# A matrix product in seven block products instead of eight, and a norm applied ahead of the transposes

## The chip, the cores and the metric

One core of one Trainium2 chip runs the whole program. The metric is device time in microseconds (us) of one execution; the kernel before takes 893.79 us in the median of three runs (893.76 to 894.05). The engines are TensorE (PE in the profile: matmuls and transposes, its weight loads are PEld), VectorE (DVE), ScalarE (ACT), GpSimd (POOL) and the queues that issue transfers (SP above all).

## The reference

The program is one encoder layer on 512 tokens of width 1024: a token mixer with recurrent head groups, a cross-attention over 256 memory tokens, and a squared-ReLU MLP, each added to the residual stream, then a final RMSNorm. What the change touches is the last third:

```python
def rmsnorm(x, g):
    y = x32 * lax.rsqrt(jnp.mean(x32 * x32, axis=-1, keepdims=True) + NORM_EPS)
    return y * g
...
x = x + cross_attention(...)                    # ends in  o @ w_xo
n = rmsnorm(x, norm_mlp)                        # 512 x 1024
x = x + jnp.square(jax.nn.relu(n @ w_up)) @ w_down   # w_up 1024 x 4096, w_down 4096 x 1024
return rmsnorm(x, norm_final)
```

## The kernel before

Everything is float32. A product is made of three matmuls on a split of each operand into a rounded high part and a low rest: high x high, high x low, low x high (`mm3`, L221 to L224). The split of a weight tile of 128 x 1024 is one copy on ACT (`wh`, L218) and one subtraction on DVE (`wl`, L219). Weight tiles come by DMA in the order of a list (`SEQ`) into three `st` buffers; `wh` and `wl` have three buffers each, so the split of tile n waits until PE has read tile n-3. `weights` splits two tiles ahead, with a raised priority.

The residual stream is held as eight tiles `xr[t, c]` (`vv` in the profile): four token tiles t of 128 tokens, two column halves c of 512. `proj_t` computes token-major tiles: four PSUM tiles (`mm`) are accumulated side by side for one column half. `proj_d` computes feature-major tiles: 128 features x 512 tokens, 24 matmuls each.

The part around the change runs so:

- **xo projection** (`proj_res`, L753): for each column half, `proj_t` yields the four token tiles; each is added to the stream on DVE (L757), squared and summed on ACT (`stats`, L751), transposed on PE in four blocks (L765) into one PSUM tile `sm`, and split into `xT` by ACT and DVE (L770, L771), scaled by the norm's gain. The factor 1/rms per token is not applied there. It commutes with ReLU, so its square (`r2`, one reciprocal at L852) is multiplied in when the MLP's output is added to the stream (L888).
- **MLP in four quarters** (L865): quarter f computes 1024 of the 4096 features, eight `proj_d` tiles of the up matrix (the *up stage*, 192 matmuls). Each is passed through ReLU on ACT (L873), squared on DVE (L874) and split (L218, L219). Then the *down stage*: `proj_t` with eight weight tiles of the down matrix, two column halves, 192 matmuls, and four additions to the stream per half (L888).
- **The end**: in the last quarter, the sums of squares, the power -0.5 on POOL (L164), the final scale and gain (L858, L861) and the output transfers.

A scheduler sets the order on each engine when the program is built. An engine takes its instructions in that order.

## Time and profile before

| | |
|---|---|
| median of the runs | 893.79 us |
| the profiled execution's own time | 895.82 us |
| its span (first to last instruction) | 894.0 us |
| PE busy | 875.6 us, 98% of the span |
| DVE busy | 497.7 us, 56% |
| ACT busy | 371.9 us, 42% |
| POOL busy | 19.5 us, 2% |
| mean granted clock of TensorE | 0.996 |

A busy time of matmuls is a pipelined one: a matmul of 512 columns is shown with some 390 ns, while the next starts 227 ns after it. What counts is the distance from start to start. The granted clock is the share of full speed that the chip allows TensorE; in this execution it is 1.00 except after the last matmul.

### The profile page before, as it was taken

What the parts mean: (1) busy time and instruction counts of PE and PEld (TensorE: products, weight loads), DVE (VectorE), ACT (ScalarE), POOL (GpSimd) and SP (SyncE); (2) the same over time, 40 slices, a digit from 0 to 9 for tenths busy, and PEclk for the clock granted to TensorE, in tenths of its full rate; (3) what the DMA queues carried; (4) which work ended last, traced back from release to release, by engine and by line L of the source; (5) the groups of instructions that cost most, each with busy time, mean ns of one, the idle gap of its engine ahead of it and who ended that gap; (6) DMA issues with size and microseconds to landing.
All of it is one profiled execution on the core that took longest, in us unless ns stands there. A gap on an engine that the chain in (4) does not pass through costs nothing.

```text
span 894.0 us, 11028 instructions
## 1 busy us (share of the span) xinstructions
PE 875.6 (98%) x4290; PEld 727.9 (81%) x4290; DVE 497.7 (56%) x863; ACT 371.9 (42%) x701; POOL 19.5 (2%) x49
## 2 busy tenths in 40 slices
PE   7999999999999999999999999999999999999996
PEld 5887888888886987888888888888888888888885
DVE  5557688679346987644555446433444344334443
ACT  5235443353358567544444445322332133114432
POOL 1000000010010000000000000000000000000001
PEclk9999999999999999999999999999999999999999
DMA  6332222312142223422212222322222233332212
GB/s 255 133 100 71 71 71 73 117 59 73 48 141 72 96 95 112 149 94 94 71 48 71 71 94 87 103 95 95 95 94 95 95 98 101 103 100 95 94 48 95
DMA packets 24614, 84.21 MB, mean 94 GB/s; under 512 B 2865, under 2 KB 2993, under 8 KB 24562
## 3 DMA queue, kind: packets, MB, share of 16 engines
q1 hardware_dynamic: 24272, 83.04, 27.5%
q8 instruction: 34, 0.56, 0.3%
q10 hardware_dynamic: 290, 0.47, 0.1%
q14 instruction: 18, 0.15, 0.1%
HBM read 81.40 MB, written 2.10 MB: 93 GB/s over the span
## 4 chain that ended last, share of the span: by engine, by line
PE 67%; DVE 1%; ACT 1%; issue 0%; POOL 0%; POOLq 0%; ACTq 0%
PE mm L223 20%; PE mm L224 20%; PE mm L222 20%; PE sm L626 2%; PE sm L611 2%; PE sm L765 1%; PE sm L223 1%; PE sm L224 1%; PE sm L222 1%; PE sm L822 0%; PE sm L596 0%; DVE wl L219 0%; DVE xT L771 0%; ACT wh L218 0%; POOL tiny L164 0%
## 5 line engine op out<-in xcount | busy, mean ns | idle before, releaser
L219 DVE TENSOR_TENSOR wl<-st,wh 128x1024 fp32r<-128x1024 f32 x141 | 172.6, 1224 | 266.5 <-ACT wh L218 263.1
L218 ACT ACTIVATE wh<-st 128x1024 fp32r<-128x1024 f32 x141 | 149.3, 1059 | 305.2 <-PE mm L224 163.2
L222 PE MATMUL mm<-xT,wh 128*128 128x512 f32 x552 | 220.0, 400 | 0.0
L223 PE MATMUL mm<-xT,wh 128*128 128x512 f32 x552 | 216.6, 392 | 0.2 <-DVE xT L771 0.2
L224 PE MATMUL mm<-xT,wl 128*128 128x512 f32 x552 | 216.8, 393 | 0.0
L224 PEld LDWEIGHTS mm<-xT,wl 128*128 128x128 f32 x552 | 103.9, 188 | 22.3 <-issue 0.6
L222 PEld LDWEIGHTS mm<-xT,wh 128*128 128x128 f32 x552 | 104.2, 189 | 21.7 <-issue 1.4
L223 PEld LDWEIGHTS mm<-xT,wh 128*128 128x128 f32 x552 | 104.2, 189 | 21.6 <-DVE xT L771 0.9
L224 PE MATMUL mm<-wh,yT 128*128 128x512 f32 x256 | 100.4, 392 | 0.0
L222 PE MATMUL mm<-wh,yT 128*128 128x512 f32 x256 | 100.2, 391 | 0.0
L223 PE MATMUL mm<-wl,yT 128*128 128x512 f32 x256 | 99.9, 390 | 0.0
L222 PE MATMUL mm<-wh,a 128*128 128x512 f32 x160 | 63.4, 396 | 0.0
L223 PE MATMUL mm<-wl,a 128*128 128x512 f32 x160 | 62.4, 390 | 0.0
L224 PE MATMUL mm<-wh,a 128*128 128x512 f32 x160 | 62.3, 389 | 0.0
L223 PEld LDWEIGHTS mm<-wl,yT 128*128 128x128 f32 x256 | 48.1, 188 | 9.8
L222 PEld LDWEIGHTS mm<-wh,yT 128*128 128x128 f32 x256 | 48.1, 188 | 9.8
L224 PEld LDWEIGHTS mm<-wh,yT 128*128 128x128 f32 x256 | 48.1, 188 | 9.6
L222 PEld LDWEIGHTS mm<-wh,a 128*128 128x128 f32 x160 | 30.1, 188 | 6.6 <-issue 0.5
L223 PEld LDWEIGHTS mm<-wl,a 128*128 128x128 f32 x160 | 30.1, 188 | 6.5 <-issue 0.5
L224 PEld LDWEIGHTS mm<-wh,a 128*128 128x128 f32 x160 | 30.0, 188 | 6.2
L373 PEld LDWEIGHTS sm<-a,t 128*128 128x128 f32 x224 | 30.1, 191 | 2.2 <-ACT t L363 0.4
L373 PE MATMUL sm<-a,t 128*128 128x128 f32 x224 | 30.9, 285 | 0.0
(222 smaller groups left out, 1110.9 us busy)
## 6 DMA issues: line engine op xcount, KB each, us to landing
st<-in_wpk SPq DMA_DIRECT2D x141, 512.0 KB, 3.2
as<-in_x SPq DMA_DIRECT2D x4, 512.0 KB, 6.4
vv<-in_x SPq DMA_DIRECT2D x8, 256.0 KB, 4.1
out<-vv SPq DMA_DIRECT2D x7, 256.0 KB, 2.2
a<-in_mem SPq DMA_DIRECT2D x2, 512.0 KB, 3.8
t<-in_rows SPq DMA_DIRECT2D x2, 256.0 KB, 5.9
gate<-in_rows SPq DMA_DIRECT2D x1, 512.0 KB, 5.2
a<-in_lmask SPq DMA_DIRECT2D x1, 448.0 KB, 8.3
```

Source lines behind the costliest of these rows:

```text
L218: sc.activation(dst_hi, src, AF.Copy)
L219: v.tensor_tensor(out=dst_lo, in0=src, in1=dst_hi.bitcast(F32), op=ALU.subtract)
L222: pe.matmul(ps, lhsT=ah, rhs=bh, start=first, stop=False)
L223: pe.matmul(ps, lhsT=ah, rhs=bl, start=False, stop=False)
L224: pe.matmul(ps, lhsT=al, rhs=bh, start=False, stop=last)
L373: pe.matmul(ps[:, z], lhsT=kc[:, z], rhs=ap(q2, w * P, [2 * L, P // (2 * L)], [512 + L, 2], [1, L]), start=True, stop=True)
L611: pe.matmul(ps, lhsT=k[:, ws * P:ws * P + P], rhs=q, start=True, stop=True)
L626: pe.matmul(ps[:, dr * 129:dr * 129 + 129], lhsT=St[:, col:col + P], rhs=mv[ws][:, h * 129:h * 129 + 129], start=(i == 0), stop=(i == len( ...
L765: pe.transpose(ps[:, k * P:k * P + P], xr[t, c][:, k * P:k * P + P], ident)
```

## The change

It has two parts.

**The down stage** of a quarter multiplies A (512 tokens x 1024 features) with B (1024 x 1024). A is cut into token halves and feature halves, B into feature halves and output halves. Eight block products of 256 x 512 x 512 become seven (P1 to P7), on sums and differences of blocks:

- S1 = A21 + A22, S2 = S1 - A11, S3 = A11 - A21, S4 = A12 - S2 and T1 = B12 - B11, T2 = B22 - T1, T3 = B22 - B12, T4 = B21 - T2
- P1 = A11 B11, P2 = A12 B21, P3 = S4 B22, P4 = A22 T4, P5 = S1 T1, P6 = S2 T2, P7 = S3 T3
- C11 = P1 + P2; C12 = P1 + P6 + P5 + P3; C21 = P1 + P6 + P7 + P4; C22 = P1 + P6 + P7 + P5

Each P takes 24 matmuls of 512 columns: two token tiles, four feature tiles, three for the split. The four T of a quarter are eight DVE subtractions of 128 x 1024 (L891 of the changed kernel), and B's raw tiles are kept for them; 14 splits of weights (*jobs*, one per P and feature pair) take the place of eight. The four S are four DVE operations of 128 x 256 per feature pair (L980 to L983). Bank X holds P1, then P1 + P6, then P1 + P6 + P7, then the whole of C21, and is read by DVE after each step (L938); Z holds P5, then P5 + P3; Y holds P2. So P6, P3, P7 and P4 wait until DVE has read the bank. The square of the ReLU moves from DVE to ACT (L965).

**The norm**: A mixes tokens of different 1/rms, so the factor can no longer be multiplied in at the end. `proj_res_norm` takes the place of `proj_res` for xo: transposes wait for the second column half, the sum of squares of the whole row, the power on POOL, and the scaling of both halves (DVE for half 0, L788; ACT for half 1, L789). The tail of the second half is `late`: each token tile ends 12 matmuls after the one before (6 in the kernel before). All 16 groups of L768's blocks come at that end, where eight of them (half 0's) lay in the matmuls of half 1 before.

```diff
+    def proj_res_norm(mat, src, tgt, st, pre):
+        for c in range(2):
+            for t, ps in proj_t(mat, 0, 512 * c, src, pre=pre if c == 0 else None, late=c == 1):
+                v.tensor_tensor(out=xr[t, c], in0=ps, in1=xr[t, c], op=ALU.add)
+                stats(st, t, c)
+                if c == 0:
+                    continue
+                s1 = tiny(1)
+                v.tensor_tensor(out=s1, in0=st[:, 2 * t:2 * t + 1], in1=st[:, 2 * t + 1:2 * t + 2], op=ALU.add)
+                r, _ = rstd_of(s1, 1, D)
+                n0, n1 = T2()[:, 0:512], T2()[:, 0:512]
+                v.tensor_scalar(out=n0, in0=xr[t, 0], scalar1=r, scalar2=None, op0=ALU.mult)
+                sc.activation(n1, xr[t, 1], AF.Copy, scale=r)
+                transp(tgt, t, 0, n0)
+                transp(tgt, t, 1, n1)
...
-    proj_res("xo", 0, os_, (x3T, V_MLP), st2, drain)
+    proj_res_norm("xo", os_, (x3T, V_MLP), st2, drain)
...
+    ORDER = ("P1", "P2", "P5", "P6", "P3", "P7", "P4")
+    JOBS = [("P1", 0), ("P2", 0), ("P1", 1), ("P2", 1)] + [(p, g) for p in ORDER[2:] for g in range(2)]
...
+        if p == "P5":
+            sub(b11, b12, b11)
+            return b11
+        if p == "P6":
+            t2 = raw[f, g, "T2"] = A4()[:, :]
+            sub(t2, b22, b11)
+            return t2
+        if p == "P7":
+            sub(b12, b22, b12)
+            return b12
+        sub(b21, b21, raw[f, g, "T2"])
+        return b21
...
+                y = T2()[:, 0:512]
+                sc.activation(y, ps, AF.Relu)
+                sc.activation(y, y, AF.Square)
...
+            v.tensor_tensor(out=s1, in0=x2_, in1=x4, op=ALU.add)
+            v.tensor_tensor(out=s2, in0=s1, in1=x1, op=ALU.subtract)
+            v.tensor_tensor(out=s3, in0=x1, in1=x2_, op=ALU.subtract)
+            v.tensor_tensor(out=s4, in0=x3_, in1=s2, op=ALU.subtract)
...
+        bank = {"P1": X, "P2": Y, "P5": Z, "P6": X, "P3": Z, "P7": X, "P4": X}
+        into = {"P1": [(0, 0)], "P2": [(0, 0)], "P5": [(2, 1)], "P6": [(0, 1)], "P3": [(0, 1)], "P7": [(2, 1)], "P4": [(2, 0)]}
...
+            w = ahead(n)
+            for u in range(2):
+                product(p, g, u, w, g == 0, g == 1)
+                if g == 1:
+                    for t0, c in into[p]:
+                        add_to(t0 + u, c, bank[p][u], fin and p in last)
```

Two places show what the change does to the order of instructions. All engines have the same order up to the tail of the xo projection.

The first is ACT at the end of the xo projection. `vv` is the residual stream, `sm` the PSUM tile of a transpose, `xT` the MLP's input, `st` and `wh` a weight tile and its high part, `t` scratch, `misc` the sums of squares, and `vv_3225` and `vv_3227` are the third and the fourth token tile. In the kernel before:

```order
L751 ACTIVATE t_775_4547,misc<-vv_3225 128x512
L770 ACTIVATE xT_4127<-sm_4505,vc 128x128
L770 ACTIVATE xT_4127<-sm_4527,vc 128x128
L218 ACTIVATE wh_4597<-st_4494 128x1024
L770 ACTIVATE xT_4127<-sm_4505,vc 128x128
L770 ACTIVATE xT_4127<-sm_4527,vc 128x128
L770 ACTIVATE xT_4127<-sm_4549,vc 128x128
L751 ACTIVATE t_777_4569,misc<-vv_3227 128x512
L770 ACTIVATE xT_4127<-sm_4571,vc 128x128
```

In the changed kernel, at the same place:

```order
L220 ACTIVATE wh_4414<-st_4412 128x1024
L773 ACTIVATE xT_4126<-sm_4496,vc 128x128
L773 ACTIVATE xT_4127<-sm_4509,vc 128x128
L220 ACTIVATE wh_4624<-st_4418 128x1024
L753 ACTIVATE t_783_4535,misc<-vv_3225 128x512
L773 ACTIVATE xT_4127<-sm_4509,vc 128x128
L789 ACTIVATE t_788_4544<-vv_3225,tiny_4541 128x512
L753 ACTIVATE t_791_4586,misc<-vv_3227 128x512
L773 ACTIVATE xT_4126<-sm_4547,vc 128x128
L789 ACTIVATE t_796_4595<-vv_3227,tiny_4592 128x512
```

The statistics of the third tile now stand behind two weight splits, of which the second reuses the buffer of the projection's last weight tile, and those of the fourth stand behind the scaling of the third.

The second place is DVE in the down stage of the second quarter (f = 1). `wl` is the low part of a weight tile, `mm` and `sm` are PSUM banks, `a`, `t` and `yT` hold the MLP's activations. In the kernel before, with the end of the up stage:

```order
L219 TENSOR_TENSOR wl_5532<-st_5505,wh_5531 128x1024
L888 SCALAR_TENSOR_TENSOR vv_3213<-mm_5437,misc,vv_3213 128x512
L888 SCALAR_TENSOR_TENSOR vv_3215<-mm_5438,misc,vv_3215 128x512
L888 SCALAR_TENSOR_TENSOR vv_3217<-mm_5439,misc,vv_3217 128x512
L888 SCALAR_TENSOR_TENSOR vv_3219<-mm_5440,misc,vv_3219 128x512
L219 TENSOR_TENSOR wl_5570<-st_5535,wh_5569 128x1024
L219 TENSOR_TENSOR wl_5600<-st_5573,wh_5599 128x1024
```

In the changed kernel, from the split of P1's second job on:

```order
L221 TENSOR_TENSOR wl_5591<-gate_5442,wh_5590 128x1024
L891 TENSOR_TENSOR a_982_5660<-as_5354,as_5265 128x1024
L891 TENSOR_TENSOR gate_5442<-gate_5476,gate_5442 128x1024
L891 TENSOR_TENSOR as_5354<-as_5354,a_982_5660 128x1024
L891 TENSOR_TENSOR a_985_5678<-a_957_5554,gate_5442 128x1024
L891 TENSOR_TENSOR gate_5476<-a_957_5554,gate_5476 128x1024
L221 TENSOR_TENSOR wl_5607<-a_954_5524,wh_5606 128x1024
L221 TENSOR_TENSOR wl_5624<-as_5265,wh_5623 128x1024
L891 TENSOR_TENSOR a_954_5524<-a_954_5524,a_985_5678 128x1024
```

The low part for P2's second feature pair (`wl_5607`) now stands behind five subtractions of raw weights; the additions of P1, P2 and P5 to the stream follow later on the same engine, behind and between five more weight splits, three splits of activations and the last four S.

## Rows read from the trace of the kernel before

**Rows 1.** The page, busy time, share of the span and instructions of each engine.

```profile
PE 875.6 (98%) x4290; PEld 727.9 (81%) x4290; DVE 497.7 (56%) x863; ACT 371.9 (42%) x701; POOL 19.5 (2%) x49
```

**Rows 2.** Timeline of PE (start, duration in us); the last row is the last matmul.

```profile
545.51 0.39 PE L222 MATMUL mm<-xT,wh 128*128 128x512 f32 x1
...
575.43 0.39 PE L222 MATMUL mm<-xT,wh 128*128 128x512 f32 x1
...
885.96 0.39 PE L224 MATMUL mm<-wh,a 128*128 128x512 f32 x1
```

**Rows 3.** All waits of PE from 380 to 886 us: total, times, longest.

```profile
PE mm L223 <- DVE xT L771: 0.2, 1, 0.2
```

**Rows 4.** Timeline from the xo projection's last matmul to the first of up.

```profile
533.76 0.42 PEld L765 LDWEIGHTS sm<-cs,vv 128*128 128x128 f32 x4 [0.31 <-DVE vv L757]
...
537.14 0.48 PE L224 MATMUL mm<-wh,yT 128*128 128x512 f32 x1
...
537.45 0.39 PE L222 MATMUL mm<-xT,wh 128*128 128x512 f32 x1
...
538.39 0.42 PEld L765 LDWEIGHTS sm<-cs,vv 128*128 128x128 f32 x4 [0.29 <-DVE vv L757]
```

**Rows 5.** Groups of instructions by line and shape: busy us, mean ns of one.

```profile
L219 DVE TENSOR_TENSOR wl<-st,wh 128x1024 fp32r<-128x1024 f32 x141 | 172.6, 1224 | 266.5 <-ACT wh L218 263.1 <-PE sm L373 3.3
L218 ACT ACTIVATE wh<-st 128x1024 fp32r<-128x1024 f32 x141 | 149.3, 1059 | 305.2 <-PE mm L224 163.2 <-PE mm L223 107.8 <-issue 31.5
L888 DVE SCALAR_TENSOR_TENSOR vv<-mm,misc,vv 128x512 f32<-128x512 f32 x32 | 23.3, 746 | 13.0 <-PE mm L224 12.8
L757 DVE TENSOR_TENSOR vv<-mm,vv 128x512 f32<-128x512 f32 x16 | 10.6, 683 | 2.3 <-PE mm L224 2.3
L770 ACT ACTIVATE xT<-sm,vc 128x128 fp32r<-128x128 f32 x64 | 20.3, 365 | 4.3 <-DVE xT L771 4.2
L771 DVE SCALAR_TENSOR_TENSOR xT<-sm,vc,xT 128x128 fp32r<-128x128 f32 x64 | 19.5, 345 | 5.8 <-ACT xT L770 5.3
L343 DVE TENSOR_SCALAR a<-a,misc 128x512 f32<-128x512 f32 x8 | 3.8, 480 | 0.0
L858 ACT ACTIVATE vv<-vv,tiny 128x512 f32<-128x512 f32 x4 | 2.8, 712 | 0.9 <-POOL tiny L164 0.9
```

**Rows 6.** Timeline of DVE where it works without a gap.

```profile
299.92 1.21 DVE L219 TENSOR_TENSOR wl<-st,wh 128x1024 fp32r<-128x1024 f32 x1
301.06 0.68 DVE L586 SCALAR_TENSOR_TENSOR yT<-t,t 128x512 f32<-128x512 f32 x1
301.66 0.41 DVE L614 TENSOR_TENSOR as<-as,sm 128x256 f32<-128x256 f32 x1
301.99 0.54 DVE L616 TENSOR_TENSOR as<-as,sm 128x384 f32<-128x384 f32 x1
```

**Rows 7.** Timeline of the end: the norm of a token tile, and an earlier power.

```profile
880.20 0.56 POOL L164 TENSOR_TENSOR tiny<-tiny,misc 128x1 f32<-128x1 f32 x1 [455.49 <-DVE tiny L162]
...
886.39 0.75 DVE L888 SCALAR_TENSOR_TENSOR vv<-mm,misc,vv 128x512 f32<-128x512 f32 x1
887.24 0.63 ACT L751 ACTIVATE t<-vv 128x512 f32<-128x512 f32 x1 [1.38 <-DVE vv L888]
887.77 0.19 ACT L751 ACTIVATION_READ_ACCUMULATOR t<-vv 128x1 f32 x1
...
888.25 0.74 DVE L861 SCALAR_TENSOR_TENSOR vv<-vv,tiny,gate 128x512 f32<-128x512 f32 x1
888.42 0.99 POOL L164 TENSOR_TENSOR tiny<-tiny,misc 128x1 f32<-128x1 f32 x1 [1.73 <-DVE tiny L162]
...
889.44 0.75 DVE L861 SCALAR_TENSOR_TENSOR vv<-vv,tiny,gate 128x512 f32<-128x512 f32 x1 [0.44 <-POOL tiny L164]
```

**Rows 8.** Stretches: from:to and length, busy time of PE, PEld, DVE, ACT, POOL, PEclk, DMA.

```profile
889.50:890.00 0.50, 0.00 (x0) 0.00 (x0) 0.50 (x1) 0.50 (x1) 0.00 (x0) 1.00 1.03 385
...
890.50:891.00 0.50, 0.00 (x0) 0.00 (x0) 0.00 (x0) 0.00 (x0) 0.00 (x0) 0.50 0.57 217
```

More of the change, by code (lines that the diff above doesn't have):

```diff
@@ L65, in _split_order @@
     for f in range(4):
-        seq += d("up", 1024 * f, 8)
-        seq += t("down", 8 * f, 0) + t("down", 8 * f, 512)
+        for j in range(4):
+            seq += d("up", 1024 * f + P * j, 1) + d("up", 1024 * f + P * (j + 4), 1)
+        for g in range(2):
+            seq += [("t", "down", 8 * f + 2 * g + k, c) for k in (0, 4) for c in (0, 512)]
     return seq
@@ L193, in load @@
     def load(i):
-        if i >= len(SEQ) or i in st_tiles:
+        if i >= len(SEQ) or i in st_tiles or SEQ[i][1] == "down":
             return
@@ L200, in split @@
     def split(i):
-        if i >= len(SEQ) or i in hl_tiles:
+        if i >= len(SEQ) or i in hl_tiles or SEQ[i][1] == "down":
             return
@@ L759, in proj_res, with transp @@
                 transp(tgt, t, c)
[L761 removed]
+    def transp(tgt, t, c, src=None):
         dst, gcol = tgt
+        src = xr[t, c] if src is None else src
         ps = smb()
         for k in range(4):
[L765 removed]
+            pe.transpose(ps[:, k * P:k * P + P], src[:, k * P:k * P + P], ident)
         for k in range(4):
@@ new lines, in trunk, with raw_load @@
+    ORDER = ("P1", "P2", "P5", "P6", "P3", "P7", "P4")
+    JOBS = [("P1", 0), ("P2", 0), ("P1", 1), ("P2", 1)] + [(p, g) for p in ORDER[2:] for g in range(2)]
+    raw, jobs_hl = {}, {}
+    def raw_load(f, n):
+        if n == 0 or n == 2:
+            t = A16()
+            raw[f, n], raw[f, n + 1] = t[:, 0:1024], t[:, 1024:2048]
+        elif n >= 4:
+            raw[f, n] = (G4() if n < 6 else A4())[:, :]
+        g, kc = divmod(n, 4)
+        i = SIDX["t", "down", 8 * f + 2 * g + 4 * (kc // 2), 512 * (kc % 2)]
+        nc.sync.dma_start(out=raw[f, n], in_=wpk[i])
@@ new lines, in source @@
+    def source(f, p, g):
+        b11, b12, b21, b22 = [raw[f, 4 * g + n] for n in range(4)]
+        sub = lambda o, a, b: v.tensor_tensor(out=o, in0=a, in1=b, op=ALU.subtract)
+        if p == "P1":
+            return b11
+        if p == "P2":
+            return b21
+        if p == "P3":
+            return b22
+        if p == "P5":
+            sub(b11, b12, b11)
+            return b11
+        if p == "P6":
[6 more added lines that the diff above has]
+        sub(b21, b21, raw[f, g, "T2"])
+        return b21
@@ new lines, in job, with finish @@
+    def job(f, n):
+        if n >= len(JOBS):
+            if f < 3:
+                split(SIDX["d", "up", 0, 1024 * (f + 1)] + n - len(JOBS))
+            return None
+        if (f, n) not in jobs_hl:
+            s_ = source(f, *JOBS[n])
+            hi, lo = T("wh", 1024, 3, F32R), T("wl", 1024, 3, F32R)
+            split_out(hi, lo, s_)
+            jobs_hl[f, n] = (hi, lo)
+        return jobs_hl[f, n]
+    def finish(t, r, first):
+        o = 1 - first
+        sc.activation(xr[t, first], xr[t, first], AF.Copy, scale=r)
+        (nc.scalar if t == 3 else nc.sync).dma_start(out=out[t * P:t * P + P, first * 512:first * 512 + 512], in_=xr[t, first])
+        z = xr[t, o]
+        v.scalar_tensor_tensor(out=z, in0=z, scalar=r, in1=gfin[:, o * 512:o * 512 + 512], op0=ALU.mult, op1=ALU.mult)
+        nc.sync.dma_start(out=out[t * P:t * P + P, o * 512:o * 512 + 512], in_=z)
@@ new lines, in trunk, with add_to @@
+    st3 = misc[:, 42:50]
+    pieces = {}
+    def add_to(t, c, ps, fin=False):
+        z = xr[t, c]
+        v.tensor_tensor(out=z, in0=ps, in1=z, op=ALU.add)
+        if not fin:
+            return
+        stats(st3, t, c)
+        if t not in pieces:
+            pieces[t] = c
+            v.tensor_tensor(out=z, in0=z, in1=gfin[:, c * 512:c * 512 + 512], op=ALU.mult)
+            return
+        s1 = tiny(1)
+        v.tensor_tensor(out=s1, in0=st3[:, 2 * t:2 * t + 1], in1=st3[:, 2 * t + 1:2 * t + 2], op=ALU.add)
+        r, _ = rstd_of(s1, 1, D)
+        finish(t, r, pieces[t])
```

113 lines of the change are left out of this document (63 added, 50 removed).

## The prediction

> **What bounds the kernel now.** I read the page first: PE is busy 98% of the span, DVE 56% and ACT 42% [rows 1]. The share alone could hide a slow PE, so I took its pace from its timeline: between two matmuls 132 apart lie 29.92 us, 0.2267 us each [rows 2]. Then PE's waits: from the xo projection to the last matmul there is one short one of 0.2 us [rows 3], and at the seam between xo and the MLP PE's weight loads wait 0.31 and 0.29 us for the stream's additions [rows 4]. So in this third of the kernel each matmul costs 0.227 us of the end, and other engines cost nothing until they are late. The question is what is late after the change.
>
> **What goes.** A quarter's down stage falls from 192 to 168 matmuls; over four quarters 96 go, and PE's order has exactly 96 rows less. 96 x 0.2267 = 21.8 us. Nothing hides this: PE waited for nothing there. The reciprocal and the multiplication by r2 were never on the path.
>
> **What the norm costs at the seam.** Before, a token tile's way from its last matmul to xT was an addition, four transposes, and eight short copies, under matmuls of its neighbours. Now it is longer, and no up matmul can start before all four token tiles have come through, since each up matmul streams all 512 tokens. I count from the start of the first token tile's last matmul (half 1), 12 matmuls or 2.72 us per tile.
>
> - One tile's chain: the addition starts 0.43 after the last matmul's start (885.96 to 886.39) and the power ends 3.02 later with a power of 0.99 [rows 2, 7]. The power took 0.56 where DVE stood still and 0.99 where L861 ran beside it [rows 7]; DVE will stand waiting for it here, so I take 0.56, and 0.06 less for the plainer addition [rows 5]: 2.5. Scaling takes 0.48 on DVE (like L343) and 0.71 on ACT (like L858) beside it [rows 5].
> - First tile: its transposes can start at 3.5. PE is through the second tile's matmuls at 2.95 and waits 0.55, since the transposes stand next in its order. The second tile's addition stands behind that scaling on DVE; PE waits another 0.7 for it. Transposes of one half hold PE some 0.42 (as in rows 4); the fourth tile's last matmul starts at 11.1 and PE is free at 11.3.
> - Third tile: it was summed long before, but on ACT its statistics stand behind a weight split that reuses the buffer the fourth tile's last matmul reads. That split runs from 11.7 to 12.8 (1.06, rows 5), the statistics to 13.4, DVE's half of the split to 14.0; then addition of the fourth tile, power to 15.8, scaling to 16.5.
> - Fourth tile: statistics 16.5 to 17.2 (ACT was scaling the third tile), power to 18.2, scaling to 18.9, transposes to 19.6. ACT and DVE may not touch one PSUM tile together, so high and low alternate, four PSUM tiles interleaved, 0.37 us per high (0.365, rows 5): the first up matmul gets its data at 20.5, the last low part is there at 25.0. In between PE can do 18 matmuls of the three up tiles whose weights lie ready (4.1 us).
>
> So PE is as far at 24.65 as if it had started at 20.55 without a gap. Its own work to there is 37 matmuls and eight groups of transposes, 11.8 us. The hole is 8.75 us; 0.6 stood there before [rows 4]; cost 8.2. By nearest rows it lies between 5 (each power hidden, splits not in the way) and 11 (every power 0.99 and no overlap between instructions).
>
> **The clock.** PE stands still for some 5 us before the third tile's transposes. At the end of this kernel the granted clock was still 1.00 at 889.5 to 890.0 and 0.50 at 890.5, four us after the last matmul had ended [rows 2, 8]. So at the seam it will probably fall to its lower level (1.2 of 2.4 GHz), and up starts there: a matmul of 0.45 instead of 0.227. No row shows how soon it comes back; I take as long as it took to fall, 4.1 us, in which 9 matmuls are done instead of 18: 2 us. The ends are 0 (it does not fall) and 16 (the first three up tiles, 72 matmuls, at half speed). The Trainium skill (TensorE: Matmul & The Clock Gate, Why this matters for your kernels) tells us to leave no longer idle gaps between bursts of matmuls, since the clock falls back in them; the rows above agree that it falls, and by that rule the seam costs its hole and then a slow start, without it only the hole.
>
> **What the products cost in a down stage.** PE needs per quarter 168 x 0.2267 = 38.1 us. DVE gets in a whole quarter 22 weight splits, 8 subtractions, some 28 smaller operations and 14 additions, about 59 us against PE's 82; as an average it keeps up. But it comes in a lump: P3 overwrites the bank of P5, and the addition that reads it is the 26th instruction from the split of P1's second job on. That split starts 1.1 us after PE's first down matmul, because its buffer comes free with the last up matmul and ACT's half takes 1.06. The 26 are 14 of 128 x 1024, 8 of 512 columns and 4 of 256. One costs 1.22, 0.68 and 0.41 by itself, but back to back they start 1.14, 0.60 and 0.33 apart [rows 5, 6]: 14 x 1.14 + 8 x 0.60 + 4 x 0.35 = 22.2, and with the start 23.3. PE needs for the four products before P3 96 x 0.2267 = 21.8. So PE loses 1.5 us by then. P4 follows P7 in one bank with six matmuls between; its read stands behind two splits on DVE, 0.4. Together 2.0 us per quarter. Bounds: 0.5 (DVE is just in time for P3) and 4.4 (each at its full duration: 25.4 against 21.8, and 0.8 at P4).
>
> In the last quarter DVE has two multiplications by the final gain more before that addition (1.2), one more wait of 0.4 between the two token tiles of P3, and before P4's bank two scalings that wait for POOL (two powers in a row, 1.4 on top): 5.0. At the end the last addition stands behind the scaling of the tile before: 0.5.
>
> The rest is hidden: up stages lose nothing, since PE runs up to four PSUM tiles ahead and each split has one whole tile, 5.4 us, for 2.3 us of work. The square on ACT runs under these matmuls. If that cover went, each late split would cost up to 2.3. DMA moves the same bytes; raw tiles come a stage ahead.
>
> **Sum**, against the profiled execution of 895.8 us (span 894.0, 1.8 around it): -21.8 + 8.2 + 2.0 + 3 x 2.0 + 5.0 + 0.5 = -0.1. The walk lets a waiting engine start 0.05 after its release; from DVE to ACT it is 0.10 (887.14 to 887.24, rows 7), some 20 times over these waits: +1.0. That is +0.9, and since the runs' median is 893.79, 2 below the profiled one, I forecast 894.7 us. Own range of this case: 889 to 901.
>
> **Rivals.**
>
> - *DVE paces the down stages.* The whole of each duration counts, not the shorter distance: 3 x 4.4 + 8 = 21 in place of 11. Then 905. It decides once the 26 instructions take over 24 us. For it: five subtractions stand in one run ahead of a split that PE needs next. Against: DVE's distances in rows 6 hold over 30 us of dense work.
> - *DVE stays ahead and the clock holds.* The additions are in time (0.5 a quarter, 2 in the last), no slow start: -21.8 + 8.2 + 3.5 + 0.5 = -9.6, so 884. For it: the margin is only 1.5 us in 22, and the clock fell only once, four us after all work, here transposes break the gap. Against: the fixed order.
> - *The clock stays low through three up tiles*: 16 instead of 2, 909. For it: in the first microseconds of up, PE waits on xT between matmuls. Against: from 25.0 on it has all data and is dense.
> - *The change does not remove the matmuls, or the scheduler fills the hole*: PE's order shows 96 rows less and nothing but the transposes in the hole. Then 872 would be possible for a filled hole; nearly excluded.
>
> **How the numbers follow.** Forecast case 0.50, DVE as pacer 0.18, DVE ahead 0.27, low clock 0.04, filled hole 0.01. A difference under 0.2% (1.8 us, so 892.0 to 895.6) can't be told from none. Of the forecast case's 0.50, its range gives 0.08 to faster, 0.21 to same, 0.21 to slower; the second rival is faster nearly whole (0.25, 0.02 same), the first and third slower. With the filled hole: faster 0.34, same 0.23, slower 0.43. The range from 883 to 905 takes in the forecast case, nearly all of the second rival and half of the first; 0.18 stays out, most of it above.
>
> **What would show it.** Right, if PE's timeline has a hole of some 8 to 11 us (less its transposes) between xo and up, with a wait for ACT's xT; if the granted clock falls there; if the 24 matmuls saved per quarter come back as waits of 1 to 3 us in each down stage, put down to DVE at the first matmul of P3 and of P4, and of 4 to 6 in the last. Wrong, if a down stage lasts over 43 or under 39 us, if the hole's length hangs on something else than ACT's order, or if the up stages show waits.

## The result, and the profile after

The changed kernel takes 896.13 us in the median of 12 runs (895.04 to 898.79); the kernel before took 894.21 us in the same session (893.76 to 895.36). The ratio is 1.0024, with a 95% interval from 1.0014 to 1.0033: 2.1 us slower. The six runs of 895.04 to 895.72 us have a mean granted clock of 0.993, the six of 896.54 to 898.79 us 0.990 to 0.992, and the profiled execution (896.54) is one of the second six. The forecast was 894.7 us, with a range from 883 to 905.

The profiled execution of the changed kernel has a span of 894.8 us, 0.7 above that of before. Its first page line beside [rows 1] says what was traded: PE works 14.7 us less and is idle more, DVE works 95 us more.

```profile
PE 860.9 (96%) x4194; PEld 711.5 (80%) x4194; DVE 592.4 (66%) x1016; ACT 434.3 (49%) x793; POOL 20.4 (2%) x53
```

PE's waits from 540 us on (engine, tile and line that waits, releaser: total, times, longest), where [rows 3] had one of 0.2 us from 380 us on:

```profile
PE sm L1006 <- DVE vv L938: 7.3, 8, 2.2
PE sm L768 <- DVE t L788: 5.7, 2, 5.2
PE sm L1007 <- DVE wl L221: 1.5, 4, 0.4
```

The stages, each from its first matmul's start to the next stage's (the front from the start of the program to a matmul shortly ahead of the xo projection, the last down stage to its last matmul's start):

| stretch | before | after | difference |
|---|---|---|---|
| front, the same instructions | 483.86 | 482.44 | -1.42 |
| xo, seam and first up stage | 97.69 | 106.06 | +8.37 |
| down stages of quarters 1 to 3 | 43.52 each | 40.94, 40.97, 41.01 | -7.64 |
| up stages of quarters 2 to 4 | 43.52 each | 43.52 each | 0 |
| last down stage | 43.29 | 44.00 | +0.71 |
| last matmul's start to the end | 8.08 | 8.78 | +0.70 |
| sum (the span) | 894.04 | 894.76 | +0.72 |

The front is no effect of the change. In the profiled execution of the kernel before, the granted clock was 0.50 from 71.2 to 74.6 us. PE had resumed at 69.42 after a wait of 1.68 us:

```profile
69.42 0.43 PE L551 MATMUL sm<-cs,a 64*128 64x64 f32 x4 [1.68 <-DVE a L540]
...
72.21 0.63 PE L223 MATMUL mm<-xT,wh 128*128 128x512 f32 x1
```

These are stretches of before (from:to and length, busy time of PE, PEld, DVE, ACT, POOL, granted clock, DMA share, GB/s):

```profile
71.00:72.00 1.00, 1.00 (x4) 0.76 (x4) 1.00 (x2) 0.84 (x2) 0.00 (x0) 0.60 0.00 0
72.00:73.00 1.00, 1.00 (x3) 0.77 (x3) 1.00 (x3) 1.00 (x1) 0.00 (x0) 0.50 0.00 0
...
74.00:75.00 1.00, 1.00 (x5) 0.83 (x4) 0.30 (x1) 0.00 (x0) 0.00 (x0) 0.69 0.90 352
```

So the statement under "Time and profile before" that the clock was 1.00 up to the last matmul is wrong. In the profiled execution of the changed kernel the same place had a wait of 1.66 us, and the clock stayed at 1.00:

```profile
69.69 0.43 PE L553 MATMUL sm<-cs,a 64*128 64x64 f32 x4 [1.66 <-DVE a L542]
```

Two profiles of the same code can differ by 1.4 us there, and comparisons below go stage by stage.

**The seam.** PE's timeline of the changed kernel (start, duration, idle time before and its releaser); 527.71 and 530.95 are the transposes of the first two token tiles, 535.07 the last matmul of xo, 540.70 and 543.15 the transposes of the third and fourth (the four rows of L768 are 32 blocks, eight groups of four, where "The change" counts 16), 544.85 the first of up, where [rows 4] had 0.31 us between the last of xo and the first of up:

```profile
527.71 1.07 PE L768 MATMUL sm<-cs,t 128*128 128x128 f32 x8 [0.45 <-DVE t L788]
...
530.95 1.10 PE L768 MATMUL sm<-cs,t 128*128 128x128 f32 x8
...
535.07 0.39 PE L226 MATMUL mm<-wh,yT 128*128 128x512 f32 x1
540.70 1.97 PE L768 MATMUL sm<-cs,t 128*128 128x128 f32 x8 [5.25 <-DVE t L788]
543.15 1.62 PE L768 MATMUL sm<-cs,t 128*128 128x128 f32 x8 [0.48 <-DVE t L788]
544.85 0.96 PE L224 MATMUL mm<-xT,wh 128*128 128x512 f32 x3
```

ACT's timeline at that place shows the third tile's statistics (536.55) behind two weight splits, and its scaling (540.16):

```profile
534.14 1.06 ACT L220 ACTIVATE wh<-st 128x1024 fp32r<-128x1024 f32 x1 [0.55 <-PE mm L226]
535.10 0.60 ACT L773 ACTIVATE xT<-sm,vc 128x128 fp32r<-128x128 f32 x2
535.60 1.05 ACT L220 ACTIVATE wh<-st 128x1024 fp32r<-128x1024 f32 x1
536.55 0.63 ACT L753 ACTIVATE t<-vv 128x512 f32<-128x512 f32 x1
...
540.16 0.72 ACT L789 ACTIVATE t<-vv,tiny 128x512 f32<-128x512 f32 x1 [2.64 <-POOL tiny L166]
```

The granted clock there (last but two in a row): it fell at 537.4, with PE standing since 535.5, and was back at 544.3.

```profile
536.00:537.00 1.00, 0.00 (x0) 0.00 (x0) 1.00 (x4) 1.00 (x2) 0.00 (x0) 1.00 0.00 0
537.00:538.00 1.00, 0.00 (x0) 0.00 (x0) 1.00 (x1) 0.52 (x3) 0.00 (x0) 0.72 0.54 119
538.00:539.00 1.00, 0.00 (x0) 0.00 (x0) 1.00 (x5) 0.00 (x0) 0.00 (x0) 0.50 0.95 381
...
544.00:545.00 1.00, 0.91 (x7) 0.68 (x6) 0.82 (x4) 0.84 (x5) 0.00 (x0) 0.87 0.00 0
```

**A down stage.** DVE's timeline in the first one: five subtractions of raw weights in a row (590.71 to 595.25), the first addition of P1 at 602.53, though PE's last matmul into P1's first bank started at 595.08, and the addition that P3 waits for, the first of the pair at 611.55. PE's row under it is P3's first matmul.

```profile
589.57 1.23 DVE L221 TENSOR_TENSOR wl<-gate,wh 128x1024 fp32r<-128x1024 f32 x1 [2.38 <-ACT wh L220]
590.71 1.22 DVE L891 TENSOR_TENSOR a<-as,as 128x1024 f32<-128x1024 f32 x1
...
595.25 1.22 DVE L891 TENSOR_TENSOR gate<-a,gate 128x1024 f32<-128x1024 f32 x1
...
602.53 0.69 DVE L938 TENSOR_TENSOR vv<-sm,vv 128x512 f32<-128x512 f32 x1
...
611.55 1.28 DVE L938 TENSOR_TENSOR vv<-sm,vv 128x512 f32<-128x512 f32 x2
```

```profile
612.39 0.47 PE L1006 MATMUL sm<-wh,yT 128*128 128x512 f32 x1 [1.05 <-DVE vv L938]
...
623.89 0.47 PE L1006 MATMUL sm<-wh,a 128*128 128x512 f32 x1 [0.38 <-DVE vv L938]
...
867.08 0.47 PE L1006 MATMUL sm<-wh,yT 128*128 128x512 f32 x1 [2.24 <-DVE vv L938]
...
880.67 0.47 PE L1006 MATMUL sm<-wh,a 128*128 128x512 f32 x1 [0.81 <-DVE vv L938]
```

The last two rows are the same two places, P3 and P4, of the last quarter. There the clock fell after the wait of 2.24 us, in the middle of matmuls, which for 3.4 us came every 0.43 us:

```profile
868.00:868.50 0.50, 0.50 (x4) 0.42 (x3) 0.50 (x2) 0.00 (x0) 0.00 (x0) 1.00 0.00 0
868.50:869.00 0.50, 0.50 (x3) 0.36 (x2) 0.50 (x2) 0.00 (x0) 0.00 (x0) 0.53 0.00 0
...
872.00:872.50 0.50, 0.50 (x4) 0.42 (x3) 0.00 (x0) 0.28 (x1) 0.00 (x0) 1.00 0.00 0
```

### The profile page after: what moved, and what is told of

It is laid out like the page before. It is cut to its first block, busy times and chain, and to the rows that moved or that the text cites. A ratio compares the mean times of both kernels' runs of the same rounds, so it can differ in the third digit from the quotient of the medians.

```text
span 894.8 us, 11089 instructions
## 1 busy us (share of the span) xinstructions
PE 860.9 (96%) x4194; PEld 711.5 (80%) x4194; DVE 592.4 (66%) x1016; ACT 434.3 (49%) x793; POOL 20.4 (2%) x53
## 4 chain that ended last, share of the span: by engine, by line
PE 54%; DVE 11%; ACT 3%; issue 2%; POOL 1%; POOLq 0%; ACTq 0%
PE mm L225 13%; PE mm L224 13%; PE mm L226 13%; DVE wl L221 5%; PE sm L1006 2%; PE sm L1007 2%; PE sm L1008 2%; ACT wh L220 2%; PE sm L628 2%; PE sm L613 2%; DVE a L891 2%; DVE vv L938 1%; PE sm L226 1%; PE sm L225 1%; PE sm L224 1%
## 5 line engine op out<-in xcount | busy, mean ns | idle before, releaser
L221 DVE TENSOR_TENSOR wl<-st,wh 128x1024 fp32r<-128x1024 f32 x109 | 133.4, 1224 | 154.1 <-ACT wh L220 150.7
L220 ACT ACTIVATE wh<-st 128x1024 fp32r<-128x1024 f32 x109 | 115.3, 1058 | 182.1 <-PE mm L225 83.7
L226 PEld LDWEIGHTS mm<-xT,wl 128*128 128x128 f32 x552 | 103.7, 188 | 22.2 <-issue 0.6
L225 PEld LDWEIGHTS mm<-xT,wh 128*128 128x128 f32 x552 | 103.9, 188 | 21.3 <-DVE xT L774 0.8
L1006 PE MATMUL sm<-wh,yT 128*128 128x512 f32 x128 | 50.3, 398 | 5.4 <-DVE vv L938 5.4
L1007 PE MATMUL sm<-wl,yT 128*128 128x512 f32 x128 | 51.1, 399 | 1.5 <-DVE wl L221 1.5
L224 PE MATMUL mm<-wh,yT 128*128 128x512 f32 x128 | 50.4, 394 | 0.0
L226 PE MATMUL mm<-wh,yT 128*128 128x512 f32 x128 | 50.3, 393 | 0.0
L225 PE MATMUL mm<-wl,yT 128*128 128x512 f32 x128 | 50.0, 391 | 0.0
L1008 PE MATMUL sm<-wh,yT 128*128 128x512 f32 x128 | 48.9, 394 | 0.0
L220 ACT ACTIVATE wh<-as 128x1024 fp32r<-128x1024 f32 x24 | 25.5, 1061 | 40.7 <-PE mm L225 21.4
L221 DVE TENSOR_TENSOR wl<-as,wh 128x1024 fp32r<-128x1024 f32 x24 | 29.4, 1224 | 16.1 <-ACT wh L220 16.1
L938 DVE TENSOR_TENSOR vv<-sm,vv 128x512 f32<-128x512 f32 x48 | 31.7, 685 | 6.4 <-PE sm L1008 6.4
L1006 PEld LDWEIGHTS sm<-wh,yT 128*128 128x128 f32 x128 | 24.3, 190 | 12.0 <-issue 4.3
```

Of the source, the lines that this page charges most:

```text
L220: sc.activation(dst_hi, src, AF.Copy)
L221: v.tensor_tensor(out=dst_lo, in0=src, in1=dst_hi.bitcast(F32), op=ALU.subtract)
L224: pe.matmul(ps, lhsT=ah, rhs=bh, start=first, stop=False)
L225: pe.matmul(ps, lhsT=ah, rhs=bl, start=False, stop=False)
L226: pe.matmul(ps, lhsT=al, rhs=bh, start=False, stop=last)
L938: v.tensor_tensor(out=z, in0=ps, in1=z, op=ALU.add)
```

## The experiments

Every kernel below the first row was run in five rounds, 4 to 11 times in all, against the kernel before on the same chip, whose medians lay between 894.14 and 895.26 us. The chips differ between groups of runs, so what is compared is the ratio, and the stages of the profiled executions. "Seam" in the table is the stretch from the matmul at 483.86 (482.44) to the first down matmul, less the 97.69 us of before.

| run | median, us | ratio to before (95%) | seam | down 1 to 3 | last down |
|---|---|---|---|---|---|
| changed kernel | 896.13 | 1.0024 (1.0014 to 1.0033) | +8.37 | 40.9 to 41.0 | 44.00 |
| norm_alone | 903.48 | 1.0102 (1.0088 to 1.0116) | +9.61 | 43.52 | 43.29 |
| products_alone | 886.61 | 0.9908 (0.9893 to 0.9923) | -0.03 | 40.9 | 42.24 |
| subs_normal | 886.06 | 0.9902 (0.9888 to 0.9915) | +9.61 | 39.1 to 39.2 | 37.98 |
| row_factor | 893.17 | 0.9985 (0.9976 to 0.9993) | +0.45 | 41.7 to 41.8 | 46.18 |
| row_factor_subs | 874.64 | 0.9781 (0.9768 to 0.9795) | +0.45 | 38.08 | 39.20 |
| stats_first | 897.35 | 1.0029 (1.0017 to 1.0040) | +8.40 | 40.9 to 41.0 | 43.96 |
| order_only | 884.96 | 0.9890 (0.9875 to 0.9905) | +8.36 | 39.1 to 39.2 | 38.00 |
| warm_hole | 895.50 | 1.0005 (0.9996 to 1.0014) | +7.77 | 40.9 | 43.95 |
| seam_manual | 897.90 | 1.0034 (1.0020 to 1.0047) | +9.44 | 40.9 | 42.27 |
| wide_parts | 896.95 | 1.0027 (1.0015 to 1.0038) | +9.06 | 41.0 | 43.96 |
| wide_stats | 896.53 | 1.0025 (1.0016 to 1.0035) | +8.70 | 40.9 to 41.0 | 43.98 |
| seam_chain | 896.78 | 1.0023 (1.0013 to 1.0033) | +9.84 | 40.9 | 42.36 |

### Each half alone

**norm_alone** is the kernel before, with the seam of the changed one.

```diff
-    proj_res("xo", 0, os_, (x3T, V_MLP), st2, drain)
+    proj_res_norm("xo", os_, (x3T, V_MLP), st2, drain)
-                v.scalar_tensor_tensor(out=z, in0=ps, scalar=r2[:, t:t + 1], in1=z, op0=ALU.mult, op1=ALU.add)
+                v.tensor_tensor(out=z, in0=ps, in1=z, op=ALU.add)
```

> The old down stage of eight products with the factor 1/rms already in xT (the changed seam alone; the multiplication by r2 is then a plain addition). Theory A (seam and products cost independently; in the changed kernel's trace the way from the xo projection to the first down matmul is 8.4 us longer than before): 894.2 + 8.4 = 902.6 us, with the same hole of some 5.3 us before the third token tile's transposes. Rival B (the hole is partly the products' doing, because the first quarter's raw tiles and splits crowd DVE and ACT there): under 899 us.

**products_alone** is the changed kernel with the seam of before; it leaves out the factor 1/rms everywhere.

```diff
-    proj_res_norm("xo", os_, (x3T, V_MLP), st2, drain)
+    proj_res("xo", 0, os_, (x3T, V_MLP), st2, drain)
```

> Seven products with the old seam; the factor 1/rms is left out of the computation altogether, which takes away its power, scaling and the order at the seam. Theory A: 896.1 - 8.4 = 887.7 us; down stages stay at 40.9 to 41.0 us in the first three quarters and 44 in the last. Rival B: with the seam gone DVE comes to the down stages with another order and the stages move by more than 1 us each. If A holds, the differences of this run and of the seam alone against the kernel before add up to the whole change within 1 us.

Both came out as theory A says: 903.48 for 902.6, 886.61 for 887.7. Only the last down stage of products_alone is shorter than expected, 42.24 us for 44, since the clock held there. The ratios give +1.02% for the norm and -0.92% for the products; their sum of +0.10% stands 1.25 us from the +0.24% of the whole, a little more than the 1 us that was expected and inside the intervals, each some 0.15% to either side. The seam's hole does not depend on the products (PE's wait of 5.2 us stands in norm_alone too), and the products' stalls do not depend on the seam.

The seam itself is 1.2 us longer in norm_alone than in the changed kernel (+9.61 against +8.37), and the clock says why. In the changed kernel it fell 2.0 us into PE's wait and was back before the first up matmul. In norm_alone it fell only at 542.1, at the end of the wait, and was back at 548.9, after 2.7 us of up matmuls:

```profile
541.00:542.00 1.00, 0.00 (x0) 0.00 (x0) 0.43 (x1) 0.43 (x1) 0.54 (x1) 1.00 0.79 262
...
548.00:549.00 1.00, 1.00 (x4) 0.72 (x4) 1.00 (x5) 0.88 (x3) 0.00 (x0) 0.53 0.00 0
```

Both times it stayed at 0.50 for 6.8 us. What that costs hangs on when it falls. subs_normal below has the late fall too (540.8 to 547.6).

### The five subtractions

**subs_normal** makes the sources of the next jobs ahead of the block with raised priority, not in it. (Raised priority lets the scheduler place instructions ahead of others.) No instruction is added or removed.

```diff
         def ahead(n):
+            for m in range(n, min(n + 3, len(JOBS))):
+                src_of(f, m)
             with tc.high_priority():
...
-            s_ = source(f, *JOBS[n])
+            s_ = src_of(f, n)
```

> The same eight subtractions of raw weights per quarter, but issued without the raised priority: two or three stand ahead of the additions of P1 and P2 on DVE, the others behind. Theory A (a down stage loses its time because P3 waits for P5's addition, which stands behind the lump of five subtractions): the waits at P3 (1.05 us, 2.24 in the last quarter) and the 0.37 for a low part go, and with the long wait of the last quarter its 3.4 us of slow clock (some 1.7 to 2.8 us): about 888 us. Rival B (the wait is the bank's hand-over itself, PE to DVE and back): no change, 896. Rival C (the work is only moved, and later weight splits come late instead): 895 to 898.

It measured 886.06, 2 us better than theory A's figure. Of PE's waits from 500 us on, those at the seam are left, and three short ones:

```profile
PE sm L768 <- DVE t L788: 6.2, 3, 5.2
PE sm L1013 <- DVE vv L945: 1.3, 3, 0.4
```

DVE's timeline in the first down stage. Between its first split (590.86) and the additions of P1 (598.57) and P2 (600.90) stands one subtraction, where the changed kernel has six (five in a row and one at 598.66); three follow at 602.10, in the wait for P5's last matmuls:

```profile
590.86 1.23 DVE L221 TENSOR_TENSOR wl<-gate,wh 128x1024 fp32r<-128x1024 f32 x1 [2.75 <-ACT wh L220]
...
593.62 1.22 DVE L891 TENSOR_TENSOR gate<-gate,gate 128x1024 f32<-128x1024 f32 x1
...
598.57 1.28 DVE L945 TENSOR_TENSOR vv<-sm,vv 128x512 f32<-128x512 f32 x2
...
600.90 1.28 DVE L945 TENSOR_TENSOR vv<-mm,vv 128x512 f32<-128x512 f32 x2
602.10 1.21 DVE L891 TENSOR_TENSOR a<-as,as 128x1024 f32<-128x1024 f32 x1
```

A down stage falls to 39.1 us, 1 us above its matmuls, and the last one from 44.0 to 38.0, with no slow clock in it. So most of the stall was DVE's order, not its amount of work and not the hand-over of a bank (rival B). Rival C comes only in the small: of the 1 us that is left, 0.6 stand at P4's first matmul and 0.3 at a low part that is late behind the moved subtractions.

### The factor without the norm ahead

**row_factor** keeps the norm out of the transposes: only tokens i and i + 256 are mixed, so the first half's factor can still be multiplied in at the end, and the second half's columns need the ratio of two factors.

```diff
+    ratio = tiny(2)
+    v.tensor_tensor(out=ratio, in0=r2[:, 2:4], in1=ms2[:, 0:2], op=ALU.mult)
+    rowf = cs[:, C_MF:C_MF + 256]
...
+            pe.matmul(ps[:, u * P:u * P + P], lhsT=ratio[:, u:u + 1].to_broadcast([P, P]), rhs=ident, start=True, stop=True)
...
                 sc.activation(y, y, AF.Square)
+                v.tensor_tensor(out=y[:, 256:512], in0=y[:, 256:512], in1=rowf, op=ALU.mult)
```

> The same function as the kernel before, with seven products and the old seam: the first token half's 1/rms squared is multiplied in at the end as before (L888's form), and the second half's columns of every squared ReLU are multiplied on DVE by the ratio of the two halves' factors, a row spread over the partitions by two small matmuls during the first up tile. Theory A (the seam costs 8.4 us because every token needs its factor before its transposes; here none does): 896.1 - 8.4 + up to 1 for 32 multiplications of 128x256 on DVE (0.33 us each, beside up matmuls) = 888 to 889. Rival B (DVE's lump starts later by these): 890 to 893.

It measured 893.17, a miss for theory A and the upper end of rival B. The seam did what A said (+0.45 in place of +8.37), but the down stages grew to 41.7, and the last one to 46.2 with a wait of 3.8 us for an addition. In the first three stages PE's longest wait is now for ACT's high part of a weight split:

```profile
PE sm L1021 <- DVE vv L950: 6.1, 5, 3.8
PE sm L1021 <- ACT wh L220: 3.5, 3, 1.2
```

The next run shows whether that is the same lump.

**row_factor_subs** is row_factor with the edit of subs_normal.

> Row factor (no norm ahead of the transposes, old seam) and the subtractions without raised priority, together. Theory A (row factor's stages of 41.7 and 46.2 us were the same lump of DVE, made longer by its own multiplications; with the lump gone they fall as they did in the changed kernel, to 39.1 and 38.0): 893.2 - 3 x 2.6 - 8.2 = 877.2 us. Rival B (the multiplications add work on DVE just where it is short): each stage keeps 1 to 2 us, 881 to 885.

It measured 874.64, 2.2% faster than the kernel before, and better than A's 877.2. The down stages are at 168 x 0.2267 = 38.1 us, and this is the only wait of PE from 540 us on, with the page's first line under it:

```profile
PE sm L1028 <- DVE tiny L164: 1.1, 1, 1.1
```

```profile
PE 853.5 (98%) x4198; PEld 709.9 (81%) x4198; DVE 603.4 (69%) x1040; ACT 430.3 (49%) x790; POOL 18.2 (2%) x49
```

DVE is busier than in any kernel before, and PE waits for it but once. The medians of that session differ by 19.7 us (894.38 and 874.64), and so do the stages (19.8, without the front): the 21.8 of the matmuls, less 0.45 at the seam, some 1.4 in the last down stage and 0.1 at the end. (The spans, 894.0 and 872.7, differ by 21.3, but 1.5 of that is the slow clock of before in the front.) So the lump was the cause here too. Why the same edit leaves 1.05 us in each down stage of subs_normal and nothing here was not tested; DVE's order differs between the two. This version beats both kernels.

### What makes the seam's hole

**stats_first** gives addition, statistics, power and scaling of a token tile at the tail a priority above the weight splits.

```diff
+                first = tc.high_priority(100000) if c else ExitStack()
+                first.__enter__()
                 v.tensor_tensor(out=xr[t, c], in0=ps, in1=xr[t, c], op=ALU.add)
                 stats(st, t, c)
...
+                first.__exit__(None, None, None)
                 transp(tgt, t, 0, n0)
```

> The changed kernel with one thing changed: at the xo projection's tail the addition, statistics, power and scaling of a token tile have a priority above the weight splits, so on ACT the statistics of the third token tile stand ahead of both splits, and on DVE the fourth tile's addition ahead of two splits. Theory A (5.25 us of the hole stand there because the third tile's statistics wait behind two splits of 1.06 and the fourth's addition behind two of 1.22): PE's wait before the third tile's transposes falls from 5.25 to under 2 us, 892 us. Rival B (the length is the norm's own chain: addition, statistics, power, scaling, transposes, and xT): at most 1 us less, 895.

It measured 897.35, a miss for theory A (892), and above rival B's 895 too. PE's timeline of this run shows the wait gone from the third tile's transposes and standing at the fourth's:

```profile
537.38 1.09 PE L768 MATMUL sm<-cs,t 128*128 128x128 f32 x8 [0.81 <-DVE t L790]
542.11 1.97 PE L768 MATMUL sm<-cs,t 128*128 128x128 f32 x8 [3.64 <-DVE xT L774]
```

Between the last xo matmul and the first of up lie 7.55 us instead of 9.78, but the first up stage takes 45.67 instead of 43.65, with the clock at 0.50 from 541.2 to 548.0: 2.2 us won, 2.0 lost.

**order_only** is stats_first with the edit of subs_normal.

> The changed kernel with the same instructions and both orders mended: subtractions without raised priority, and a token tile's norm ahead of the splits at the seam. Theory A (independent): 886.1 less what the seam's order alone brings (some 4 us), 882 us.

It measured 884.96 where 882 was expected. Its ratio of 0.9890 is 1.1 us better than that of the subtractions' order alone (0.9902), and its seam 1.25 us shorter, but the two intervals overlap. Nearly all that it wins over the changed kernel comes from the subtractions.

**warm_hole** puts 20 matmuls more into PE's hole.

```diff
+                if c == 1 and t == 3:
+                    warm = mmb()
+                    xh = src[0][0][:, 0:P]
+                    for i in range(20):
+                        pe.matmul(warm, lhsT=xh, rhs=src[0][0], start=True, stop=True)
```

> The changed kernel with 20 more matmuls of 128x512 into a spare bank, whose result nobody reads, in PE's hole between the last xo matmul and the third token tile's transposes (20 x 0.2267 = 4.5 us of the 5.25). Theory A (the granted clock falls there because PE stands still, and what it costs is the slow transposes, 1.97 and 1.62 us for eight against 1.07 at full clock, and where it comes back late, up to 1.25 us of the first up stage, as in two other runs): 896.1 - 1.4 - up to 1.2 = 893.5 to 894.7 us, with a granted clock of 1.00 through the seam. Rival B (ACT and DVE set the pace there, and the clock costs nothing): 896.

It measured 895.50, by itself nearer to rival B's 896 than to A's 893.5 to 894.7. By the ratios, 1.0005 where the changed kernel has 1.0024, it is 1.7 us less, which lies between A's 1.4 and 2.6; but the two intervals touch, so the time alone does not decide. The trace does: the clock stays at 1.00 through the seam, the transposes take 1.09 us for eight, the first up stage 43.65:

```profile
535.05 4.70 PE L784 MATMUL mm<-yT 128*128 128x512 f32 x20
540.44 1.09 PE L768 MATMUL sm<-cs,t 128*128 128x128 f32 x8 [0.69 <-DVE t L793]
542.88 1.09 PE L768 MATMUL sm<-cs,t 128*128 128x128 f32 x8 [1.35 <-DVE t L793]
```

The seam still costs 7.77 us at full clock: that is what the norm's chain costs in this order of ACT and DVE.

**seam_manual** has DVE's and ACT's order at the tail written by hand.

```diff
+            with tc.manual_schedule(engines={mybir.EngineType.DVE, mybir.EngineType.Activation}):
...
+                    if t == 2:
+                        parts(0, 1)
+                    summed(t, ps)
+                    if t == 3:
+                        scaled(2)
+                    power(t)
+                    if t == 2:
+                        split(up1)
+                    if t != 2:
+                        scaled(t)
+                parts(2, 3)
```

> The changed kernel with the order of DVE and ACT written out by hand at the xo projection's tail: third token tile's addition and statistics first, one weight split in the wait for its power, then the fourth tile's addition and statistics, both scalings, the parts of xT for both tiles together, and the next weight split only behind them. The run with raised priority moved the wait from the third tile's transposes (5.25 to 0.81 us) to the fourth's (0.48 to 3.64), because the fourth's statistics and power still stood behind one split on ACT and two on DVE; and the first up stage took 45.7 us in place of 43.7, with the clock at 0.50 for six us of it. Theory A (with no split in the way, the last xo matmul to the first up matmul takes the norm's own chain, some 6 us in place of 9.8, and PE's stand is then too short for the clock to fall): 896.1 - 3.8 = 892 us. Rival B (the clock falls all the same, and what is gained in the hole is lost in the first up stage): 894 to 896.

It measured 897.90, a miss for both theories. The order by hand is the reason: the 16 pairs of high and low parts of the first two tiles now stand in one block ahead of the third tile's addition, and PE waits 6.3 us.

**wide_parts** makes the high and the low part of xT with one instruction each per half, and leaves out the norm's gain there. **wide_stats** adds the edit of stats_first. What both share:

```diff
+            sc.activation(hi, p3, AF.Copy)
+            v.tensor_tensor(out=lo, in0=p3, in1=hi.bitcast(F32), op=ALU.subtract)
```

> The changed kernel with the high and low parts of xT written as one ACT and one DVE instruction per transposed tile of 128x512 instead of four each of 128x128; the norm's gain, a factor per block that needs the four, is left out of the computation at this place. The run with the order written by hand had the wait again (6.3 us), this time behind 16 pairs of parts of 0.39 us each (530.3 to 536.9). Theory A (three orders gave nearly the same seam because ACT and DVE have some 4.5 us of serial work per token tile there, 3.1 of them the eight pairs of parts, against PE's 2.72: work, not order, makes most of the hole): some 1.9 us per tile instead of 3.1, four tiles, so 3 to 5 us less in all: 891 to 893. Rival B (the order of the splits makes the hole): the wait of 5.2 us stays, at most 1.5 us less, 895.

> The same wide parts (gain left out), with the raised priority of each token tile's norm at the seam, so that the splits stand behind the third tile's statistics. Theory A: as the run before or up to 2 us better, 890 to 892. Rival B (order alone): 892 here against 895 there.

Both miss A (896.95 and 896.53). In wide_parts weight splits still hold the third tile back, one on ACT ahead of its statistics and two on DVE ahead of its power (a wait of 4.6 us); wide_stats has 3.7 us at the fourth. Fewer parts alone bring nothing, and neither rival's pair of numbers fits.

**seam_chain** is written by hand once more, with each of these out of the chain at once.

```diff
+                    elif t == 2:
+                        summed(t, ps)
+                        parts(1, 2, 4)
+                        power(t)
+                        parts(1, 4, 8)
+                    else:
+                        v.tensor_tensor(out=xr[t, 1], in0=ps, in1=xr[t, 1], op=ALU.add)
+                        scaled(2)
+                        stats(st, t, 1)
+                        power(3)
```

> The changed kernel with the xo projection's tail written out by hand a second time, with all its parts of xT and its gain. So far each single relief left the seam as long: splits behind the third tile's statistics (wait moved to the fourth tile), one long block of parts ahead of the third tile (6.3 us of wait again), half the parts (4.6 us of wait, the splits again). Here every one of these stands out of the chain's way at once: parts of the second tile in the waits for POOL, the third tile's addition as soon as PE has done it, the fourth's before the third's scaling, one split in the wait for the fourth's power and the next behind everything. Theory A (the hole has several causes of nearly one length, and only all of them together give it back): third transposes about 1.5 us after the last xo matmul, fourth 2.5 behind, first up matmul about 6 us after the last xo matmul where it was 9.8, and the clock may hold: 896.1 - 3.7 = 892.4 us, 893.5 if the clock falls. Rival B (the chain of one token tile, addition to transposes and parts, is itself as long as the hole): 895 or more.

It measured 896.78, a miss for theory A; rival B's 895 or more came. Third and fourth transposes stand at 3.8 and 5.8 us after the last xo matmul (534.45). The fourth are a little earlier than in any other order (5.9 in stats_first), the third are not (1.2 there):

```profile
538.25 1.49 PE L813 MATMUL sm<-cs,t 128*128 128x128 f32 x8 [3.42 <-DVE t L808]
...
540.21 1.97 PE L813 MATMUL sm<-cs,t 128*128 128x128 f32 x8 [0.46 <-DVE t L808]
```

But the clock is at 0.50 from 538.8 to 549.0, a wait of 1.1 us for a part of xT comes on top, and the first up stage takes 46.33 us. Stretches of that run, the granted clock last but two:

```profile
541.00:542.00 1.00, 1.00 (x6) 0.77 (x4) 0.82 (x4) 0.42 (x2) 0.00 (x0) 0.50 0.00 0
548.00:549.00 1.00, 1.00 (x3) 0.73 (x3) 0.32 (x1) 0.00 (x0) 0.00 (x0) 0.50 0.00 0
549.00:550.00 1.00, 1.00 (x6) 0.80 (x5) 0.00 (x0) 0.00 (x0) 0.00 (x0) 0.98 0.67 201
```

So with the norm ahead of the transposes the seam costs 8.4 to 9.8 us in every order tried, and 7.8 with the clock held up. Each relief moved the wait to the next link (third tile's statistics, fourth tile's power, a block of parts) or gave it back as slow matmuls. What the order by hand would bring with the clock held up by idle matmuls was not tried, and the share of either stays open. Taking the chain out of the way of PE altogether (row_factor) is what removes the cost.

## Why the forecast came out as it did

**The time** was 1.4 us off, and the net of the terms 1.2. That is in part luck, for larger errors cancel: the seam cost 1.8 us less than forecast, and 1.0 us for hand-overs was counted on top; the down stages cost 3.8 us more, and the tail 0.2. Point by point, where "the walk" is the prediction's count from instruction to instruction:

- *21.8 us of matmuls go.* Right: a down stage without waits takes 38.08 us in row_factor_subs against 43.52, 5.44 x 4 = 21.8.
- *Seam: 8.2 for the hole, 2.0 for the clock.* Measured: 8.37 for both in this execution, 9.61 in two others with the same seam. Counted from the first token tile's last matmul (524.15), the walk had the first transposes at 3.5 and the first up matmul at 20.5; they stand at 3.56 and 20.70. It had the third tile's power at 15.8 and the fourth's scaling at 18.9; they end at 15.98 and 19.2. In part these agree by chance: the walk had the fourth transposes done at 19.6 and then a wait for xT, where at the slow clock they ended at 20.6 and PE did not wait for xT. The mis-sized term is the clock's: it fell as forecast, but most of the time at 0.50 passed while PE stood or transposed. warm_hole puts a price of 0.6 us on it in the seam of this execution and 1.8 against the two others, whose first up stage began slow (44.9 us). The prediction says that no row shows how soon the clock comes back, and that it fell only once. The trace of before had both: 3.4 us at 0.50 (71.2 to 74.6), which cost 1.4 us against the changed kernel's front.
- *Mechanism of the hole.* Half right. The third tile's statistics did stand behind two splits, as the walk said, and PE waited 5.25 us for them. But the prediction's test "wrong, if the hole's length hangs on something else than ACT's order" has come out against it: with that order mended (stats_first) the way from the last xo matmul to the first of up fell by 2.2 of 9.8 us only, since the fourth tile's chain and the parts are nearly as late, and the slow start of up took those 2.2 back. The rows of one execution show which link was last, not what comes without it.
- *Down stages: 2.0 us each, and some of the 1.0 of hand-overs.* Measured 40.97 - 38.08 = 2.9. The wait at P3 costs 1.2 (forecast 1.5) and that at P4 0.54 (0.4), as named. Not forecast: the lump also makes a low part of a weight split late, 0.37 us of wait and 0.53 of time, and the remaining 0.6 are smaller gaps at the first matmuls behind such splits.
- *Last quarter: 5.0.* Measured 44.00 + 0.23 - 38.08 = 6.1, of which 1.7 are the slow clock after P3's wait (products_alone and the two runs by hand had the same waits, no slow clock, and 42.2 to 42.4). Without it 4.4. A wait of 2.24 us that brings the clock down was not in the walk. The other terms are off both ways: P3's wait costs 2.4 (forecast 2.7) and P4's 1.0 (1.8), the wait of 0.4 between P3's two token tiles did not come, and the late low part and smaller gaps (0.9) were not forecast.
- *Tail: 0.5.* Measured 0.70.
- *The rivals.* DVE as pacer (905) did not come: DVE's rows of 128 x 1024 in the lump start 1.13 to 1.14 us apart, as [rows 6] said, and the 26 instructions take 22.7 us (22.2 forecast). Clock low through three up tiles did not come in this execution; seam_chain is the run nearest to it, 2.7 us. DVE ahead (884) did not come either, but subs_normal shows how near it was: the same instructions in another order measured 886, with the clock falling at the seam all the same.
- *The other signs.* The 9.8 us between xo and up, the fall of the clock there, the waits at P3 and P4 and up stages without waits (43.52) came as named. Three came out otherwise: PE did not wait for ACT's xT in the hole but for DVE's scaling (L788), the waits in the last down stage sum to 3.4 us (4 to 6 forecast), and that stage took 44.0 us, over the 43 that the prediction had named as a sign against it.

The Trainium skill (TensorE: Matmul & The Clock Gate, Why this matters for your kernels) says not to leave long idle gaps between bursts of matmuls. The runs agree with its direction: in every seam with the norm ahead the clock fell, in the hole or within 0.6 us behind it, but for the one filled with matmuls. In size the rows decide: after waits of 1.68 and 2.24 us, neither of them long beside the hole, it fell too, in the kernel before at 71.2 us and in the changed kernel at 868.5.

## What to carry to other kernels

A saving on the bound engine is worth what the other engines let through in the stage where it falls: here 21.8 us of matmuls came to nothing, because a norm stood between two dense stages and because raised priority had put five subtractions in front of the additions that free a PSUM bank. Before a factor is moved ahead of transposes, ask whether it commutes with what follows up to a ratio; and when work is issued ahead, look at what stands behind it on the same engine, since average load (69% of DVE in the fastest version) says nothing about it. If one link of a serial chain is relieved and the wait moves on to the next, stop tuning its order and take the chain off the path.

## What had not been expected of the hardware

- The granted clock fell in the midst of dense matmuls, 868.5 us, though PE had resumed at 867.08 after a wait of 2.24 us. It came back at 871.9. For that time a matmul of 512 columns took 0.43 us from start to start.
- The same wait brings the clock down in one execution and not in another: seam_manual has the wait of 2.2 us at P3 too, and its clock held through a last stage of 42.27 us. The same holds of the waits of 1.68 us (before) and 1.66 us (changed kernel) near 69 us.
- How long the clock stayed at 0.50 at the seam differed between runs of nearly one seam: 6.8 us in the changed kernel (537.4 to 544.3), 10.2 in seam_chain (538.8 to 549.0), where PE had resumed earlier, at 538.25. Where it fell late in PE's wait, as in norm_alone, the slow time lay on the up matmuls.
